# Two heads' products on TensorE issued as one group in five attention stages

## The chip, the cores and the metric

The kernel runs on one core of one Trainium2 chip, as one program. The metric is device time in microseconds (us) of one execution; for the kernel before, the median of three runs is 3418.66 us.

## What is computed

The reference passes a sequence of 512 tokens of width 1024 through three transformer blocks, one after the other. What matters here are the five attentions in which two heads share the 128 rows or the 128 columns of the PE array:

- **fox** (block 1): eight heads of width 64, causal, with a forget-gate bias. A head's scores are `q[64, 128] . k[64, n]` with n = 128, 256, 384 or 512 keys, then a softmax, then the product with the values.
- **da** (block 2, differential attention): eight heads, each with two score maps of contraction 64 over all 512 keys; the second map's softmax is subtracted from the first's with a weight.
- **wa** (block 2, window attention): sixteen heads of width 64 over a window of 256 or 384 keys, with a sink, then `values[128, 64]` products.
- **na** (block 3, neighbourhood attention): eight heads of width 64 over 256 keys, then values.
- **mla** (block 3, latent attention): eight heads with scores of contraction 96 over 512 keys, then values of width 64.

```
s = jnp.einsum('bhqd,bhkd->bhqk', q, k, preferred_element_type=jnp.float32) * scale
p = jax.nn.softmax(...)
o = jnp.einsum('bhqk,bhkd->bhqd', p.astype(v.dtype), v)
```

Around them lie dense projections (each fp32 weight is split into a high and a low part, and three products are summed) and two mixtures of experts.

## The kernel before

The kernel is written with a tile framework. It is traced as straight code without loops at run time; when the program is built, a list scheduler fixes the order of every engine's instructions: of the instructions that are ready in its own model of time it takes the one with the best priority, which is by default the earliest in the trace. On the chip each engine takes its queue in exactly that order. So an instruction of a later dense projection can stand between two instructions of an attention, and work of an earlier part comes ahead of a later part's.

An attention stage is a row of parts, one for each pair of heads and each block of 128 queries; `stagger` runs the first half of part n+1 (scores and softmax) before the second half of part n (transposes and values). In each part:

- `self.sc()` hands out the one score tile in PSUM (`bufs=1`, two banks of 512 floats): head 0's scores go to bank 0, head 1's to bank 1.
- The score products are lines L649 (fox), L1434 (da), L1513 (wa) and L1816 (na). Head 0 uses rows 0 to 63 of the array and head 1 rows 64 to 127; the profile gives such a product the form 64*128. Each fp32 product of the source appears as two MATMUL instructions, so a pair of heads is four.
- `softmax2` reads the scores on VectorE (L459, head 0 and then head 1), takes exponentials on ScalarE (L468), and in wa and na divides on VectorE (L476).
- `transposes` (L433 on TensorE) turns the probabilities; the copies out of PSUM are L436 on VectorE and L438 on ScalarE. In wa and mla one head's copy is on VectorE and the other's on ScalarE; in na both heads come with one copy on ScalarE.
- The value products are L1532 (wa), L1828 (na) and L1930 (mla). Both heads use all 128 rows; head 0 writes from columns 0 to 63 and head 1 from columns 64 to 127 of the array (form 128*64). For each block of 128 keys the source issues head 0 and then head 1. The values of fox (L662) and da (L1447) use the whole array (form 128*128) and are not touched.
- Dense work that the scheduler puts between: L419, L1277 and L383.

In the source the two score products of a part stand next to each other, but nothing keeps other TensorE work from being ordered between them.

Of the kernel before, what the change touches and what calls it, by code (L numbers as in the profile page):

```python
# [35 lines left out]
P = 128  # L36
# [91 lines left out]
class Net:  # L128
# [55 lines left out]

    def pst(self):
        return self.ps.tile([P, 512], F32, name="pst", bufs=2)

    def keep_warm(self, x, n):

# [330 lines left out]
    def mixer1(self):  # L520
# [9 lines left out]
        with ExitStack() as cx:  # L530
# [104 lines left out]
            def fox_part(hp, qt):  # L635
                n = (qt + 1) * P
                if qt == 0:
                    ftab[hp] = tab = A.tile([P, 2, S], F32, name="ftab")
                    for i in range(2):
                        pb = self.pst()  # L640
                        h = 2 * hp + i
                        nc.tensor.matmul(pb, self.ident[:8, h:h + 1].to_broadcast([8, P]), cs[:8], start=True,
                                         stop=True)
                        nc.scalar.activation(tab[:, i], pb, AF.Copy, scale=-1.0)
                tab = ftab[hp]
                sp = self.sc()
                for i in range(2):
                    hs = slice(i * 64, i * 64 + 64)
                    nc.tensor.matmul(sp[:, i, :n], fq[hp][hs, qt * P:n], fk[hp][hs, :n], start=True, stop=False)  # L649
                for i in range(2):  # L650
                    nc.tensor.matmul(sp[:, i, qt * P:n], idb, mb, start=False, stop=True)
                e = A.tile([P, 2, S], F32, name="e", bufs=2)
                _, rl = self.softmax2([e[:, i, :n] for i in range(2)], [sp[:, i, :n] for i in range(2)], 1.0,
                                      tabs=[tab[:, i, :n] for i in range(2)], normalize=False)
                yield
                po = self.pst()
                for i in range(2):
                    h = 2 * hp + i
                    eT = A.tile([P, 4, P], F32, name="eT", bufs=3)
                    self.transposes(eT, e[:, i], qt + 1)  # L660
                    for k in range(qt + 1):
                        nc.tensor.matmul(po[:, i * 64:(i + 1) * 64], eT[:, k], fv[k][:, h * 64:(h + 1) * 64],  # L662
                                         start=(k == 0), stop=(k == qt))
                nc.vector.tensor_mul(y[:, qt, hp * P:(hp + 1) * P].rearrange("p (i d) -> p i d", i=2),
                                     po[:, :P].rearrange("p (i d) -> p i d", i=2),
                                     rl.unsqueeze(2).to_broadcast([P, 2, 64]))
                if qt < 3:
                    return
                o = y[:, :, hp * P:(hp + 1) * P].rearrange("p a (i d) -> p a i d", i=2)
                sq = A.tile([P, 4, 2, 64], F32, name="gy")  # L670
                nc.scalar.activation(sq, o, AF.Square)
                ss = self.small.tile([P, 4, 2], F32, name="ss8")
                nc.vector.reduce_sum(ss, sq, axis=AX.X)
                r = self.power(ss.rearrange("p a i -> p (a i)"), 8, 64, EPS)
                nc.vector.tensor_mul(o, o, r[:, :8].rearrange("p (a i) -> p a i", a=4).unsqueeze(3).to_broadcast([P, 4, 2, 64]))
# [653 lines left out]
    def mixer2(self):  # L1329
# [96 lines left out]
        def da_part(h, qt):  # L1426
            slope = 2.0 ** -(h + 1)
            if qt == 0:
                rows_da[h] = E.tile([P, 4, P], F32, name="oh", bufs=1)
            tab = dist[:, 384 - qt * P:896 - qt * P]  # L1430
            sp = self.sc()
            for m in range(2):
                ms = slice(m * 64, (m + 1) * 64)
                nc.tensor.matmul(sp[:, m], dq[h][ms, qt * P:(qt + 1) * P], dk[h][ms], start=True, stop=True)  # L1434
            e = e_tile()
            l, rl = self.softmax2([e[:, m] for m in range(2)], [sp[:, m] for m in range(2)], slope,
                                  tabs=[tab] * 2, normalize=False)
            c = self.small.tile([P, 1], F32, name="dac")
            nc.vector.scalar_tensor_tensor(c, l[:, 0:1], rl[:, 1:2], nlam, op0=OP.mult, op1=OP.mult)
            nc.vector.scalar_tensor_tensor(e[:, 0], e[:, 1], c, e[:, 0], op0=OP.mult, op1=OP.add)  # L1440
            yield
            oh = rows_da[h]
            eT = E.tile([P, 4, P], F32, name="eT", bufs=3)
            self.transposes(eT, e[:, 0], 4, eng="a")
            po = self.pst()
            for k in range(4):
                nc.tensor.matmul(po[:, :P], eT[:, k], dv[h][:, k], start=(k == 0), stop=(k == 3))  # L1447
            nc.scalar.activation(oh[:, qt], po[:, :P], AF.Copy, scale=rl[:, 0:1])
            if qt < 3:
                return  # L1450
            sq = E.tile([P, 4, P], F32, name="eT", bufs=3)
            nc.gpsimd.tensor_mul(sq, oh, oh)
            ss = self.small.tile([P, 4], F32, name="ss4")
            nc.vector.reduce_sum(ss, sq, axis=AX.X)
            r = self.power(ss, 4, P, EPS)
            nc.vector.tensor_mul(oh, oh, r[:, :4].unsqueeze(2).to_broadcast([P, 4, P]))
            pt = self.pst()
            for a in range(4):
                nc.tensor.transpose(pt[:, a * P:(a + 1) * P], oh[:, a], self.ident)
            o_da[h] = O()  # L1460
            nc.scalar.activation(o_da[h], pt, AF.Copy, scale=sg)
# [41 lines left out]
        def wa_part(c2, i, qt):  # L1503
# [4 lines left out]
            n, t0 = k1 - k0, k0 - (qt * P - P)  # L1508
            nb = n // P
            sp = self.sc()  # L1510
            for j in range(2):
                gs = slice(j * 64, j * 64 + 64)
                nc.tensor.matmul(sp[:, j, :n], wq[c2 * 4 + i][gs, qt * P:(qt + 1) * P], wk[c2][gs, k0:k1],  # L1513
                                 start=True, stop=True)
            e = e_tile()
            self.softmax2([e[:, j, :n] for j in range(2)], [sp[:, j, :n] for j in range(2)],
                          [float(sl[h]) for h in hs], tabs=[wd[:, t0:t0 + n]] * 2,
# [7 lines left out]
            for j in range(2):  # L1525
                self.transposes(eT[j], e[:, j], nb, eng="a" if j else "v")
            po = self.pst()
            for k in range(nb):
                kt = k0 // P + k
                for j in range(2):  # L1530
                    g = 2 * c2 + j
                    nc.tensor.matmul(po[j * 64:(j + 1) * 64, :P], wv[kt // 2][:, kt % 2, g * 64:(g + 1) * 64],  # L1532
                                     eT[j][:, k], start=(k == 0), stop=(k == nb - 1))
            for j, h in enumerate(hs):
                (nc.scalar.copy if j else nc.vector.tensor_copy)(o_wa[h // 2][r0, qt * P:(qt + 1) * P],
                                                                 po[j * 64:(j + 1) * 64, :P])
# [207 lines left out]
    def mixer3(self, after):  # L1744
# [63 lines left out]
        def na_part(hp, j):  # L1808
            if j == 0:
                tabs_na[hp] = na_tabs(hp)  # L1810
            tabs = tabs_na[hp]
            sp = self.sc()
            for hh in range(2):
                hs = slice(hh * 64, hh * 64 + 64)
                kv = k[hp][hs].rearrange("p (i c) -> p i c", c=64)
                nc.tensor.matmul(sp[:, hh, :256], q[hp][hs, j * P:(j + 1) * P], kv[:, :, starts[j]:starts[j] + 32],  # L1816
                                 start=True, stop=True)
            e = N.tile([P, 2, 256], F32, name="ne", bufs=2)
            self.softmax2([e[:, i] for i in range(2)], [sp[:, i, :256] for i in range(2)], 1.0,
                          tabs=[t[:, j].rearrange("p i c -> p (i c)") for t in tabs])  # L1820
            yield
            eT = N.tile([P, 4, P], F32, name="neT", bufs=2)
            self.transposes(eT, e.rearrange("p i k -> p (i k)"), 4, eng="a")
            po = self.pst()
            for kk in range(2):
                for hh in range(2):
                    h = 2 * hp + hh
                    nc.tensor.matmul(po[hh * 64:hh * 64 + 64, :P], vw[j][kk][:, h * 64:(h + 1) * 64],  # L1828
                                     eT[:, hh * 2 + kk], start=(kk == 0), stop=(kk == 1))
            nc.vector.tensor_copy(o_na[hp].rearrange("p (r j c) -> p j r c", j=4, r=8)[:, j],  # L1830
                                  po[:, :P].rearrange("p (r c) -> p r c", r=8))

# [70 lines left out]
        def mla_part(hp, qt):  # L1903
# [20 lines left out]
            for b in range(2):  # L1924
                self.transposes(eT[:, b], e[:, b], 4, eng="a" if b else "v")
            po = self.pst() if hp == 0 else self.acc()
            for kt in range(4):
                for b in range(2):
                    h = 2 * hp + b
                    nc.tensor.matmul(po[b * 64:(b + 1) * 64, :P], mv[:, kt, h * 64:(h + 1) * 64], eT[:, b, kt],  # L1930
                                     start=(kt == 0), stop=(kt == 3))
            nc.scalar.copy(o_ml[hp][:, qt * P:(qt + 1) * P], po[:, :P])

        heads = {}
# [126 lines left out]
```

## Time and profile before

| | |
|---|---|
| Median of 3 runs | 3418.66 us (3416.3 to 3419.46) |
| The profiled execution | 3424.08 us, its span 3422.2 us |
| TensorE busy | 3242.2 us, 95% of the span |
| VectorE, ScalarE busy | 1636.8 us (48%), 1289.1 us (38%) |
| Chain that ended last | PE 75%, DMA 13%, VectorE 6%, ScalarE 2% |

PE is TensorE, DVE VectorE and ACT ScalarE. A row of the timeline has start, duration, engine, line, operation, tiles, form and count; consecutive instructions of one kind are merged into one row. Matmuls are pipelined: a row's duration overlaps the next row's, so what a group costs is read from its start to the next row's start. Idle time before an instruction stands in brackets with what ended it.

### The profile page before, as it was taken

The numbers are of one execution on the slowest core, as the hardware profiler recorded it, in microseconds if no ns is written. First come the engines' busy times: TensorE is split into PE (matmuls) and PEld (weight loads), VectorE is DVE, ScalarE is ACT, GpSimd is POOL, SyncE is SP. The second block draws the span as 40 slices with busy tenths as digits, with TensorE's granted clock in tenths as the row PEclk, the third lists the DMA queues.
The fourth block names the chain that finished last, engine by engine and source line by source line (L and its number), as shares of the span: only waits on it lengthen the run. The fifth ranks groups of instructions, "written<-read, shape, count | busy, mean of one in ns | idle before, by whom it ended". The sixth has DMA issues, their size and how long they took to land.

```text
span 3422.2 us, 41346 instructions
## 1 busy us (share of the span) xinstructions
PE 3242.2 (95%) x15500; PEld 2092.0 (61%) x15500; DVE 1636.8 (48%) x3520; ACT 1289.1 (38%) x2662; POOL 130.4 (4%) x128
## 2 busy tenths in 40 slices
PE   8999989998999999999999998898888999999998
PEld 6777866667767767668634333232224676788886
DVE  5546789998354454656311111011014446573356
ACT  6334658886344353554100000000003344452244
POOL 0010010002000000000000000000000000000000
PEclk9999989999999999999899999999999999999999
DMA  5115479985112212114799999999997312133243
GB/s 169 58 62 141 148 261 376 373 313 199 62 50 72 73 53 87 50 35 171 269 402 420 422 420 422 421 421 423 420 422 272 98 50 68 62 99 99 80 165 137
DMA packets 212938, 713.96 MB, mean 209 GB/s; under 512 B 20144, under 2 KB 28096, under 8 KB 180352
## 3 DMA queue, kind: packets, MB, share of 16 engines
q1 hardware_dynamic: 190272, 668.38, 51.1%
q10 hardware_dynamic: 19520, 32.43, 3.0%
q0 software_dynamic: 2944, 10.49, 1.0%
q8 instruction: 123, 2.02, 0.2%
q14 instruction: 79, 0.65, 0.1%
HBM read 693.68 MB, written 17.56 MB: 208 GB/s over the span
## 4 chain that ended last, share of the span: by engine, by line
PE 75%; DMA 13%; DVE 6%; ACT 2%; issue 1%; POOL 1%; ACTq 0%; SPq 0%; POOLq 0%; DVEq 0%
PE acc L419 23%; PE acc L1662 8%; PE acc L282 7%; PE acc L1085 5%; PE acc L1277 5%; PE acc L1693 3%; PE acc L1107 2%; PE pst L433 2%; DMA xl<-in_w_exp_up_dram 2%; DMA rawx<-in_w_exp_gate_dram 2%; DMA xl<-in_w_exp_down_dram 2%; PE sc L1625 2%; PE acc L367 2%; DMA rawx<-in_w_exp_down_dram 2%; DVE wl L221 1%
## 5 line engine op out<-in xcount | busy, mean ns | idle before, releaser
L221 DVE TENSOR_TENSOR wl<-raw,wh 128x512 fp32r<-128x512 f32 (+3 forms) x910 | 606.6, 683 | 578.0 <-ACT wh L218 525.1
L218 ACT CAST wh<-raw 128x512 fp32r<-128x512 f32 (+3 forms) x910 | 546.5, 612 | 737.8 <-PE acc L419 491.4
L419 PE MATMUL acc<-xh,wh 128*128 128x512 f32 x1072 | 426.4, 398 | 7.1 <-ACT wh L218 5.0
L419 PE MATMUL acc<-xl,wh 128*128 128x512 f32 x1072 | 425.0, 396 | 0.0
L419 PE MATMUL acc<-xh,wl 128*128 128x512 f32 x1072 | 424.4, 396 | 0.0
L1662 PE MATMUL acc<-rawx,xe 128*64 128x512 f32 x1256 | 293.0, 601 | 29.3 <-DMA rawx<-in_w_exp_up_dram 20.9
L419 PEld LDWEIGHTS acc<-xh,wh 128*128 128x128 f32 x1072 | 202.2, 189 | 61.0 <-issue 10.2
L419 PEld LDWEIGHTS acc<-xl,wh 128*128 128x128 f32 x1072 | 202.4, 189 | 51.5 <-issue 13.2
L419 PEld LDWEIGHTS acc<-xh,wl 128*128 128x128 f32 x1072 | 202.2, 189 | 50.4 <-issue 10.8
L1662 PEld LDWEIGHTS acc<-rawx,xe 128*64 128x64 f32 x1256 | 84.2, 137 | 228.2 <-issue 147.7
L1693 PE MATMUL acc<-rawx,wh 128*64 128x512 f32 x640 | 147.0, 599 | 13.1 <-DMA rawx<-in_w_exp_down_dram 13.0
L282 PE MATMUL acc<-wl,xsh 128*128 128x512 f32 x336 | 132.9, 396 | 4.8 <-DVE wl L221 4.7
L207 POOL TENSOR_TENSOR pw_r<-pw_v,halfneg 128x1 f32<-128x1 f32 (+2 forms) x64 | 58.4, 913 | 2053.8 <-DVE pw_v L206 2036.2
L282 PE MATMUL acc<-wh,xsl 128*128 128x512 f32 x336 | 132.2, 394 | 0.0
L282 PE MATMUL acc<-wh,xsh 128*128 128x512 f32 x336 | 128.7, 392 | 0.0
L1662 PE MATMUL acc<-raw,xe 128*64 128x512 f32 x512 | 119.2, 598 | 9.6 <-DMA raw<-in_w_exp_gate_dram 9.6
L1681 DVE SCALAR_TENSOR_TENSOR wl<-wl,acc 128x512 f32<-128x512 f32 x32 | 22.0, 687 | 205.0 <-PE acc L1662 205.0
L468 ACT ACTIVATE e<-e,smx 128x512 f32<-128x512 f32 (+3 forms) x160 | 98.7, 618 | 50.1 <-DVE smx L466 37.3
L438 ACT COPY wh<-pst 128x512 f32<-128x512 f32 x32 | 18.7, 585 | 260.1 <-PE pst L433 260.0
L1693 PEld LDWEIGHTS acc<-rawx,wh 128*64 128x64 f32 x640 | 42.1, 136 | 103.7 <-issue 68.5
L1085 PE MATMUL acc<-wh,xeh 128*96 128x512 f32 x256 | 103.6, 406 | 0.7 <-ACT xeh L218 0.7
L1085 PE MATMUL acc<-wl,xeh 128*96 128x512 f32 x256 | 103.6, 404 | 0.0
(538 smaller groups left out, 5581.3 us busy)
## 6 DMA issues: line engine op xcount, KB each, us to landing
rawx<-in_w_exp_up_dram SPq DMA_DIRECT2D x80, 1024.0 KB
rawx<-in_w_exp_down_dram SPq DMA_DIRECT2D x80, 1024.0 KB
rawx<-in_w_exp_gate_dram SPq DMA_DIRECT2D x77, 1024.0 KB
raw<-in_w_in_dram SPq DMA_DIRECT2D x58, 1024.0 KB
raw<-in_w_exp_gate_dram SPq DMA_DIRECT2D x34, 1024.0 KB
raw<-in_w_exp_down_dram SPq DMA_DIRECT2D x32, 1024.0 KB
raw<-in_w_exp_up_dram SPq DMA_DIRECT2D x30, 1024.0 KB
raw<-in_w_ffn_out_dram SPq DMA_DIRECT2D x22, 1024.0 KB
```

The source lines that it names most:

```text
L218: nc.scalar.copy(hi, src)
L221: nc.vector.tensor_sub(lo, src, hi.bitcast(F32))
L282: nc.tensor.matmul(acc[a, hf], l[:, js], r, start=(k == 0 and q == 0), stop=(k == nk - 1 and q == 2))
L367: self.nc.tensor.matmul(acc[a], l[:, k, js], r[:, :n], start=(k == 0 and q == 0), stop=(k == nk - 1 and q == 2))
L419: nc.tensor.matmul(outs[j], l, r, start=(kk == 0 and q == 0), stop=(kk == nk - 1 and q == 2))
L433: nc.tensor.transpose(pt[:, k * P:(k + 1) * P], src[:, (b + k) * P:(b + k + 1) * P], self.ident)
L468: nc.scalar.activation(es[i], src[i], AF.Exp, bias=nm[:, i:i + 1], scale=sc[i], accum_out=l[:, i:i + 1])
L1085: nc.tensor.matmul(ps, l[:, k], r, start=(k == 0 and q == 0), stop=(k == 7 and q == 2))
L1107: nc.tensor.matmul(py[hf], l[:, k], r, start=(k == 0 and q == 0), stop=(k == 3 and q == 2))
L1277: nc.tensor.matmul(acc[j], l[:, js], r, start=(k == 0 and q == 0), stop=(k == nk - 1 and q == 2))
L1662: nc.tensor.matmul(acc[f // 2][f % 2 * 64:(f % 2 + 1) * 64], cur[:, k, es], raw[f], start=(k == 0), stop=(k == 7))
L1693: nc.tensor.matmul(py[hf * 64:(hf + 1) * 64], uT[ab][:, kk, c * 64:(c + 1) * 64], raw[:, d, hf * 512:(hf + 1) * 512], start=(i + d == 0), ...
```

## The change

A helper `together` takes a list of calls. It makes the first, and then makes the others inside two contexts: `issue_after(mm.ins)` puts an edge of order on TensorE from the first instruction to each of the others (issue order only, no wait for its end), and `high_priority()` gives the others a better priority than any ordinary instruction. It is used for the scores of fox, da, wa and na, each with head 1 first and head 0 behind it, and for the values of wa, na and mla, where for each block of keys head 1 now comes ahead of head 0. The arithmetic, the tiles, the buffers and every other engine's instructions stay. mla's scores, fox's mask product (L651) and the values of fox and da stay as they are.

```diff
+    def together(self, calls):
+        mm = calls[0]()
+        with self.tc.issue_after(mm.ins), self.tc.high_priority():
+            for c in calls[1:]:
+                c()
...
-                for i in range(2):
+                def scores(i):
                     hs = slice(i * 64, i * 64 + 64)
-                    nc.tensor.matmul(sp[:, i, :n], fq[hp][hs, qt * P:n], fk[hp][hs, :n], start=True, stop=False)
+                    return nc.tensor.matmul(sp[:, i, :n], fq[hp][hs, qt * P:n], fk[hp][hs, :n], start=True, stop=False)
+
+                self.together([lambda: scores(1), lambda: scores(0)])
...
-            for k in range(nb):
-                kt = k0 // P + k
-                for j in range(2):
-                    g = 2 * c2 + j
-                    nc.tensor.matmul(po[j * 64:(j + 1) * 64, :P], wv[kt // 2][:, kt % 2, g * 64:(g + 1) * 64],
-                                     eT[j][:, k], start=(k == 0), stop=(k == nb - 1))
+            def values(k, j):
+                g, kt = 2 * c2 + j, k0 // P + k
+                return nc.tensor.matmul(po[j * 64:(j + 1) * 64, :P], wv[kt // 2][:, kt % 2, g * 64:(g + 1) * 64],
+                                        eT[j][:, k], start=(k == 0), stop=(k == nb - 1))
+
+            self.together([lambda k=k, j=j: values(k, j) for k in range(nb) for j in (1, 0)])
```

The scores of da, wa and na change as those of fox do, and the values of na and mla as those of wa.

## Rows read from the trace of the kernel before

**Rows 1.** The profile's page: the span, and the busy time of each engine (share of the span, number of instructions).

```profile
span 3422.2 us, 41346 instructions
...
PE 3242.2 (95%) x15500; PEld 2092.0 (61%) x15500; DVE 1636.8 (48%) x3520; ACT 1289.1 (38%) x2662; POOL 130.4 (4%) x128
```

**Rows 2.** Busy time by stretch: start:end and length in us, then busy us (and instructions) of PE, PEld, DVE, ACT and POOL, the granted clock, the DMA share and GB/s. The stretches are fox with what runs between its parts, two of da, three of wa, one of na and one of mla.

```profile
100.00:260.00 160.00, 158.95 (x854) 112.76 (x852) 84.51 (x231) 54.42 (x124) 12.94 (x10) 0.96 0.18 57
964.00:1037.00 73.00, 69.25 (x321) 41.91 (x320) 47.84 (x133) 38.50 (x93) 6.16 (x6) 1.00 0.09 30
1176.00:1258.00 82.00, 78.34 (x418) 51.58 (x416) 54.63 (x161) 47.96 (x124) 6.14 (x6) 1.00 0.20 65
1302.00:1320.00 18.00, 18.00 (x93) 11.22 (x92) 11.26 (x48) 10.89 (x33) 0.00 (x0) 1.00 0.18 59
1373.00:1436.00 63.00, 63.00 (x343) 37.39 (x342) 41.81 (x161) 37.62 (x118) 0.00 (x0) 1.00 0.06 18
1441.00:1520.00 79.00, 78.93 (x415) 45.45 (x414) 53.63 (x210) 43.41 (x142) 3.00 (x2) 1.00 0.11 37
2694.00:2763.00 69.00, 68.96 (x392) 42.70 (x391) 45.13 (x183) 33.97 (x94) 0.00 (x0) 1.00 0.15 43
2893.00:2952.00 59.00, 54.05 (x367) 35.26 (x366) 34.78 (x72) 26.32 (x69) 0.00 (x0) 0.94 0.02 5
```

**Rows 3.** Timeline of PE in da: a pair of heads in one piece (x4), one in two pieces (x2 and x2, the first such pair of the stage), one behind an idle stretch, and the end of the last pair in two pieces.

```profile
965.40 1.13 PE L1434 MATMUL sc<-qkv 64*128 64x512 f32 x4
966.46 0.50 PE L419 MATMUL acc<-xh,wh 128*128 128x512 f32 x1
966.80 0.39 PE L419 MATMUL acc<-xl,wh 128*128 128x512 f32 x1
967.03 0.40 PE L419 MATMUL acc<-xh,wl 128*128 128x512 f32 x1
...
972.27 1.12 PE L1434 MATMUL sc<-qkv 64*128 64x512 f32 x2
973.33 1.16 PE L1447 MATMUL pst<-qkv,eT 128*128 128x128 f32 x8
974.41 1.12 PE L1434 MATMUL sc<-qkv 64*128 64x512 f32 x2
975.47 0.50 PE L419 MATMUL acc<-xh,wh 128*128 128x512 f32 x1
...
991.80 1.12 PE L1434 MATMUL sc<-qkv 64*128 64x512 f32 x2 [0.73 <-DVE smx L459]
...
1253.88 1.12 PE L1434 MATMUL sc<-qkv 64*128 64x512 f32 x2
```

**Rows 4.** Timeline of PE in wa: one part's scores in two pieces, the values of another part in two pieces (x2 and x6), and the first and the last split of each kind in the stage.

```profile
1308.17 0.91 PE L1513 MATMUL sc<-qkv 64*128 64x384 f32 x2
...
1310.43 0.43 PE L1532 MATMUL pst<-eT,qkv 128*64 128x128 f32 x2
...
1448.85 0.91 PE L1513 MATMUL sc<-qkv 64*128 64x384 f32 x2
1449.69 0.66 PE L433 MATMUL pst<-c_ident,e 128*128 128x128 f32 x4
1450.28 0.91 PE L1513 MATMUL sc<-qkv 64*128 64x384 f32 x2
1451.12 0.43 PE L1532 MATMUL pst<-eT,qkv 128*64 128x128 f32 x2
1451.48 0.50 PE L419 MATMUL acc<-xl,wh 128*128 128x512 f32 x1
1451.81 0.40 PE L419 MATMUL acc<-xh,wl 128*128 128x512 f32 x1
1452.14 0.65 PE L1532 MATMUL pst<-eT,qkv 128*64 128x128 f32 x6
1452.72 0.50 PE L419 MATMUL acc<-xh,wh 128*128 128x512 f32 x1
...
1504.73 0.91 PE L1513 MATMUL sc<-qkv 64*128 64x384 f32 x2
...
1516.30 0.43 PE L1532 MATMUL pst<-eT,qkv 128*64 128x128 f32 x2
```

**Rows 5.** Timeline of PE in na: one piece of a split pair of scores with what follows it, and a part's values in one piece (x8) with what follows them.

```profile
2732.98 0.70 PE L1816 MATMUL sc<-nk,nq 64*128 64x256 f32 x2
2733.60 0.65 PE L433 MATMUL pst<-c_ident,ne 128*128 128x128 f32 x4
...
2735.94 0.66 PE L1828 MATMUL pst<-neT,vw 128*64 128x128 f32 x8
2736.53 0.66 PE L433 MATMUL pst<-c_ident,ne 128*128 128x128 f32 x4
```

**Rows 6.** Timeline of PE in fox: the first half of a split pair of scores over 512 keys, and the values that follow it.

```profile
120.64 1.12 PE L649 MATMUL sc<-t 64*128 64x512 f32 x2
121.69 0.66 PE L662 MATMUL pst<-t,eT 128*128 128x64 f32 x4
```

**Rows 7.** What PE waited for in da (964 to 1260 us): total us, times, longest.

```profile
PE sc L1434 <- DVE smx L459: 3.9, 6, 0.8
```

**Rows 8.** Timeline of DVE in wa: the first read of the scores whose second piece began at 1450.28.

```profile
1451.22 0.56 DVE L459 CUSTOM_DVE_ANT_0 e<-sc,c_wdist 128x384 f32<-128x384 f32 x1 [0.63 <-PE sc L1513]
```

More of the change, by code (lines that the diff above doesn't have):

```diff
@@ L1431, in da_part, with scores @@
             sp = self.sc()
-            for m in range(2):
+            def scores(m):
                 ms = slice(m * 64, (m + 1) * 64)
-                nc.tensor.matmul(sp[:, m], dq[h][ms, qt * P:(qt + 1) * P], dk[h][ms], start=True, stop=True)
+                return nc.tensor.matmul(sp[:, m], dq[h][ms, qt * P:(qt + 1) * P], dk[h][ms], start=True, stop=True)
+            self.together([lambda: scores(1), lambda: scores(0)])
             e = e_tile()
@@ L1510, in wa_part, with scores @@
             sp = self.sc()
-            for j in range(2):
+            def scores(j):
                 gs = slice(j * 64, j * 64 + 64)
-                nc.tensor.matmul(sp[:, j, :n], wq[c2 * 4 + i][gs, qt * P:(qt + 1) * P], wk[c2][gs, k0:k1],
-                                 start=True, stop=True)
+                return nc.tensor.matmul(sp[:, j, :n], wq[c2 * 4 + i][gs, qt * P:(qt + 1) * P], wk[c2][gs, k0:k1],
+                                        start=True, stop=True)
+            self.together([lambda: scores(1), lambda: scores(0)])
             e = e_tile()
@@ L1527, in wa_part @@
             po = self.pst()
-            for k in range(nb):
-                kt = k0 // P + k
-                for j in range(2):
-                    g = 2 * c2 + j
-                    nc.tensor.matmul(po[j * 64:(j + 1) * 64, :P], wv[kt // 2][:, kt % 2, g * 64:(g + 1) * 64],
-                                     eT[j][:, k], start=(k == 0), stop=(k == nb - 1))
+            def values(k, j):
[3 more added lines that the diff above has]
+            self.together([lambda k=k, j=j: values(k, j) for k in range(nb) for j in (1, 0)])
             for j, h in enumerate(hs):
@@ L1812, in na_part, with scores @@
             sp = self.sc()
-            for hh in range(2):
+            def scores(hh):
                 hs = slice(hh * 64, hh * 64 + 64)
                 kv = k[hp][hs].rearrange("p (i c) -> p i c", c=64)
-                nc.tensor.matmul(sp[:, hh, :256], q[hp][hs, j * P:(j + 1) * P], kv[:, :, starts[j]:starts[j] + 32],
-                                 start=True, stop=True)
+                return nc.tensor.matmul(sp[:, hh, :256], q[hp][hs, j * P:(j + 1) * P],
+                                        kv[:, :, starts[j]:starts[j] + 32], start=True, stop=True)
+            self.together([lambda: scores(1), lambda: scores(0)])
             e = N.tile([P, 2, 256], F32, name="ne", bufs=2)
@@ L1824, in na_part, with values @@
             po = self.pst()
[L1825 to L1829, printed above, removed]
+            def values(kk, hh):
+                h = 2 * hp + hh
+                return nc.tensor.matmul(po[hh * 64:hh * 64 + 64, :P], vw[j][kk][:, h * 64:(h + 1) * 64],
+                                        eT[:, hh * 2 + kk], start=(kk == 0), stop=(kk == 1))
+            self.together([lambda kk=kk, hh=hh: values(kk, hh) for kk in range(2) for hh in (1, 0)])
             nc.vector.tensor_copy(o_na[hp].rearrange("p (r j c) -> p j r c", j=4, r=8)[:, j],
@@ L1926, in mla_part, with values @@
             po = self.pst() if hp == 0 else self.acc()
[L1927 to L1931, printed above, removed]
+            def values(kt, b):
+                h = 2 * hp + b
+                return nc.tensor.matmul(po[b * 64:(b + 1) * 64, :P], mv[:, kt, h * 64:(h + 1) * 64], eT[:, b, kt],
+                                        start=(kt == 0), stop=(kt == 3))
+            self.together([lambda kt=kt, b=b: values(kt, b) for kt in range(4) for b in (1, 0)])
             nc.scalar.copy(o_ml[hp][:, qt * P:(qt + 1) * P], po[:, :P])
```

## The prediction

> **What bounds the kernel now.** I read the page first: PE is busy for 3242.2 of 3422.2 us, VectorE for less than half of it [rows 1]. But a share over the whole span is a mean over unlike stages, so next I read the busy time stage by stage [rows 2], and only then the timeline of PE inside the stages that the change touches [rows 3 to 6]. Three kinds of stage are to be seen there. In wa PE has no idle time to speak of (18.00 of 18, 63.00 of 63, 78.93 of 79 us); the same holds for na (68.96 of 69), and fox is close (158.95 of 160). There, a microsecond of PE that is not needed is a microsecond off the end, for dense projections stand ready behind the attention and move up. In da PE is idle for 3.75 of 73 and 3.66 of 82 us: a few waits for the softmax, at the change from one head to the next [rows 2, 3, 7]. In mla it is idle for 4.95 of 59.
>
> **What a pair costs whole and in pieces.** In da, a pair in one piece (x4, all four matmuls of both heads) runs from 965.40 to the next instruction at 966.46, 1.06 us. One head alone (x2) runs from 972.27 to 973.33, again 1.06 us, and the other head, separated by the value products of the part before, from 974.41 to 975.47, once more 1.06 [rows 3]. So two heads side by side take what one takes, and a split pair pays twice. There is also an **edge**: the dense matmul right behind such a block takes 0.34 us to its successor (966.46 to 966.80) where its neighbour takes 0.23 (966.80 to 967.03), 0.11 more [rows 3]; the one right ahead of a block also takes 0.33 (1451.81 to 1452.14 in wa) [rows 4]. One block fewer thus saves up to two edges, 0.2 us, where full-array work stands on both sides, and nothing where another half-array block is the neighbour.
>
> The first rule to hold against this is in the Trainium skill, *TensorE: Matmul & The Clock Gate*, section on packing small matmuls: a weight load overlaps with running matmuls only when its row group differs. That fits the scores, whose heads lie in different rows, but the values of wa, na and mla share all 128 rows and differ in columns alone; by that rule joining them would save nothing. The rows disagree: a lone x2 of values takes 0.36 us (1451.12 to 1451.48), four such would be 1.44, and x8 in na takes 0.59 (2735.94 to 2736.53) [rows 4, 5]. I go by the rows and keep the rule as a rival below.
>
> **The terms, part by part.** The change removes no instruction and adds none; it only closes gaps in PE's order. I counted the split pairs in the timeline and price each by its shape.
>
> - *Fox scores.* 16 parts; those with 384 and 512 keys are all split, 4 + 4. A lone 384 piece is 0.84 us (in wa, 1448.85 to 1449.69 [rows 4]), a lone 512 piece 1.05 (120.64 to 121.69 [rows 6]). 4 x 0.84 + 4 x 1.06 + 8 x 0.2 for edges = 9.2 us.
> - *Da scores.* 14 of 32 pairs are split, the first at 972.27, the last ending with the piece at 1253.88 [rows 3]. 14 x (1.06 + 0.2) = 17.6 us.
> - *Wa scores.* 19 of 32, the first at 1308.17, the last second half at 1504.73: 14 of 384 keys and 5 of 256 [rows 4]. A lone 256 piece is 0.62 (2732.98 to 2733.60, in na [rows 5]). 14 x 1.04 + 5 x 0.82 = 18.7 us.
> - *Wa values.* 30 of 32 parts put head 0's first product (x2) ahead of the rest, from 1310.43 to 1516.30 [rows 4], because its transposed probabilities come first. Price: 0.36 + 0.58 (the x6, 1452.14 to 1452.72) - 0.59 (the x8) = 0.35, and 0.2 of edges where full-array work stands between. In 11 of the 30 a piece touches a score block, so no edge: 19 x 0.55 + 11 x 0.35 = 14.3 us.
> - *Na.* 5 of 16 score pairs of 256 keys are split: 5 x 0.82 = 4.1 us. All 16 value groups are already whole [rows 5]: nothing.
> - *Mla values.* 6 of 16 are split in the same way: 6 x 0.35 = 2.1 us.
>
> On PE this is 66.0 us in all, the upper bound of what shorter PE work can give.
>
> **What of it reaches the end.** Fox and na: all, 9.2 and 4.1, since PE is the bound there and na, whose values are all whole and most of whose pairs are, shows a stage in the new form with PE full [rows 2]. Da: 6 of the 14 split pairs follow an idle wait of PE (such as 991.80 behind 0.73 us of idle; six waits, 3.9 us [rows 3, 7]); there a free PE is worth nothing, so I take the other 8, 10.1 us, with 0 and 17.6 as the ends. Wa: 33.0 us less of 160 leaves 127. VectorE's 106.7 us (11.26 + 41.81 + 53.63) would then be 84% of it, not 67%, so some waits must appear. I let PE idle as much as in da, 3.75 of 73 or 5.1%: 6.5 us, which leaves 26.5. Mla: PE already waits, I take half, 1.0. Sum: 9.2 + 10.1 + 26.5 + 4.1 + 1.0 = **50.9 us**.
>
> What is moved, and what hides it: head 0's product no longer runs as soon as it can. Both products now wait for the later bank, which VectorE gives back one pass later (0.56 us for 384 keys [rows 8]). In PE's queue that wait would stand ahead of everything; the order set at build time puts dense work before it, as around the split pairs now [rows 4]. On the other side a cost goes that the sum doesn't count: VectorE reads the scores only when the second piece is done (the second piece ends at 1451.12, the read starts at 1451.22 after 0.63 us of idle for it [rows 4, 8]), so a pair in one piece releases the softmax earlier. At most this takes away da's whole idle time, 3.75 + 3.66 = 7.4 us. No DMA is issued by the moved work, and SP's and POOL's queues keep their instructions; the dense work that moves up needs its weights earlier, but the DMA share in these stretches is 0.02 to 0.20 [rows 2], so I price that at nothing.
>
> **The rivals.**
>
> - *VectorE and the softmax chain become the bound.* In da, VectorE's share is 66% (47.84 of 73) and PE already waits; wa stands at 67% [rows 2]. If that is the share at which these chains no longer shorten, PE merely idles in da and wa, and fox and na are all that is left: 13.3 us, 3405. For it: VectorE's waits for scores show how tightly the two engines take turns. Against: na at 65% (45.13 of 69) and wa at 67% run with PE full, so the share alone does not force waits. The Trainium skill says the same in *TensorEngine Tiling (Array Packing)*, PSUM bottleneck: tiling speeds up TensorE but not the reading of PSUM, which may become the limit. By that page the time would be this rival's.
> - *Only the values gain nothing,* by the rule on row groups above: the wa values' 14.3 at the 80% that I keep of wa (26.5 of 33.0), 11.5, and mla's 1.0 go: 3380. The x8 row speaks against it [rows 5].
> - *Slower: the front product stalls the queue.* 96 pairs (16 + 32 + 32 + 16) each wait up to one VectorE pass, 0.56 us: 54 us. 48 value groups (32 + 16) wait for the second copy, up to the 1.02 us between the first piece and the rest (1451.12 to 1452.14 [rows 4]): 49 us. If nothing covers these, 103 - 66 = 37 us slower, 3455. It decides from the point at which more than 64% of them (66 of 103) is uncovered. Against: PE now has dense work to put there.
> - *It does not join them.* The edge says "behind", not "next"; if head 0's product is not ready in the order's planning, something else still goes between, and the time stays, 3419.
>
> **How the numbers follow.** The profiled execution took 3424.08 us, 5.4 more than the median of the runs; with 50.9 less it would take 3373.2. On the median: 3418.66 - 50.9 = **3368**. Chances: this case 0.70, the chain as bound 0.14, the values' rule 0.04, nothing joined 0.06, slower 0.06. Low end: all 66.0 of PE and da's 7.4 of idle, 3345. High end: the chain as bound, 3406. That leaves out "nothing joined", "slower" and part of the first rival, some 0.19. A measurement of this kernel can tell about 0.2% (7 us) from no change; by these cases faster has 0.88, the same 0.06, slower 0.06.
>
> **What would show it.** In the timeline of the changed kernel every score block of da, wa, fox and na should be x4 and every value block whole, each as long as a whole block now (1.06 for 512 keys). The stretches of fox, da, wa and na should be shorter by the terms above. PE's idle time in wa should be 3 to 10 us: near zero would mean that I held back too much, above 20 that the softmax chain has taken over. VectorE's waits for L1513 should shrink. It would be wrong if x2 rows remain, or if PE idles ahead of the joined blocks with a VectorE release.

## The result and the profile after

The kernel with the change takes 3378.19 us (median; 3374.8 to 3379.03), the kernel before, timed beside it, 3417.48 (3414.68 to 3419.46): a ratio of 0.9882 [0.9869, 0.9894], 39.3 us faster. The forecast was 50.9 us, 3368, with a range of 3345 to 3406: the sign and the range hold, and the size is 11.6 us too large. The profiled execution of the kernel after took 3379.03 us (its span 3377.0), near its median; that of the kernel before lies 6.6 above its own, so the two spans differ by 45.2.

The lines of code are 8 to 22 further down in the kernel after: scores L657 (fox), L1445 (da), L1527 (wa), L1834 (na); values L1547 (wa), L1848 (na), L1952 (mla); `transposes` L441 with copies L444 (VectorE) and L446 (ScalarE); softmax L467; dense L427; da's transposes at the end of a head L1472 (before: L1459).

The page: span, and busy time of each engine, to be read against [rows 1].

```profile
span 3377.0 us, 41353 instructions
PE 3182.9 (94%) x15500; PEld 2067.6 (61%) x15500; DVE 1634.4 (48%) x3520; ACT 1291.0 (38%) x2662; POOL 130.9 (4%) x128
```

The same 15500 matmuls take 59.3 us less of PE, and the span is 45.2 shorter: PE is idle more than before. Where, the busy times by stretch say (columns as in [rows 2]; the stretches cover about the same parts of da, da, wa, wa, wa, na and mla, as the numbers of instructions show):

```profile
950.40:1025.00 74.60, 64.94 (x320) 42.02 (x319) 47.77 (x133) 39.29 (x93) 6.19 (x6) 0.95 0.09 29
1162.30:1246.00 83.70, 74.57 (x432) 52.53 (x431) 54.85 (x166) 49.86 (x129) 7.19 (x7) 0.98 0.15 51
1288.50:1305.60 17.10, 16.88 (x94) 10.86 (x93) 11.29 (x48) 11.02 (x33) 0.00 (x0) 1.00 0.19 62
1358.60:1410.00 51.40, 49.95 (x340) 32.09 (x339) 41.12 (x161) 37.38 (x118) 0.00 (x0) 1.00 0.06 22
1416.00:1482.50 66.50, 64.28 (x422) 40.81 (x421) 53.73 (x210) 43.93 (x144) 3.00 (x2) 1.00 0.12 40
2652.40:2717.50 65.10, 65.06 (x392) 41.30 (x391) 45.34 (x183) 34.36 (x94) 0.00 (x0) 1.00 0.17 50
2848.00:2906.50 58.50, 50.90 (x358) 31.86 (x357) 33.75 (x72) 26.94 (x69) 0.00 (x0) 1.00 0.02 6
```

In wa, 135 us now do what 160 did, with PE idle for 0.22 + 1.45 + 2.22 = 3.9 us; na is 65.1 for 69 and still full. The two stretches of da are no shorter than before, PE idle there has risen from 3.75 and 3.66 to 9.66 and 9.13 us, and the mean clock is under 1.00.

The timeline of PE in the kernel after: whole blocks in fox and wa.

```profile
116.71 1.13 PE L657 MATMUL sc<-t 64*128 64x512 f32 x4
117.77 0.66 PE L672 MATMUL pst<-t,eT 128*128 128x64 f32 x4
...
1425.99 0.66 PE L1547 MATMUL pst<-eT,qkv 128*64 128x128 f32 x8 [0.56 <-ACT eT L446]
1426.58 0.50 PE L427 MATMUL acc<-xl,wh 128*128 128x512 f32 x1
...
1427.24 0.70 PE L1527 MATMUL sc<-qkv 64*128 64x256 f32 x4
1427.87 0.87 PE L441 MATMUL pst<-c_ident,e 128*128 128x128 f32 x6
```

Each takes from its start to the next row what a whole block, or one half of a split pair, took before: 1.06 us for 512 keys, 0.63 for 256 (a lone half took 0.62 [rows 5]), 0.59 for x8. All 96 score pairs and the 48 value groups of wa and na are in one piece.

To say where the gain arises I take the starts of the n-th matmul on PE in both traces (both have 15500) and give after minus before; a stage's gain is the change of that difference over the stage. The difference at the start of fox (-3.0) stems from the start-up, before any changed instruction.

| Stage | after - before at its start and end, us | gain | forecast |
|---|---|---|---|
| fox and the output projection behind it | -3.0, -13.1 | 10.1 | 9.2 |
| da | -13.75, -13.4 | -0.35 | 10.1 |
| wa | -13.4, -39.7 | 26.3 | 26.5 |
| na | -41.6, -45.7 | 4.1 | 4.1 |
| mla | -45.6, -45.2 | -0.4 | 1.0 |

Outside the changed stages the difference wanders, by up to 3.4 us from one trace to another. The sums of fox, wa and na are near their forecasts, and da's is missing whole. What these sums are made of is told below; in fox and in wa errors of opposite sign cancel.

### The profile page after: what moved, and what is told of

Its sections match the earlier page's. It is cut to its first block, busy times and chain, and to the rows that moved or that the text cites. A ratio compares the mean times of both kernels' runs of the same rounds, so it can differ in the third digit from the quotient of the medians.

```text
span 3377.0 us, 41353 instructions
## 1 busy us (share of the span) xinstructions
PE 3182.9 (94%) x15500; PEld 2067.6 (61%) x15500; DVE 1634.4 (48%) x3520; ACT 1291.0 (38%) x2662; POOL 130.9 (4%) x128
## 4 chain that ended last, share of the span: by engine, by line
PE 53%; DMA 13%; DVE 6%; ACT 3%; issue 1%; POOL 1%; ACTq 0%; POOLq 0%; SPq 0%; DVEq 0%
PE acc L427 19%; PE acc L1679 8%; PE acc L290 5%; PE acc L1287 5%; PE acc L1710 4%; DMA rawx<-in_w_exp_gate_dram 3%; DMA xl<-in_w_exp_up_dram 3%; DMA xl<-in_w_exp_down_dram 3%; PE sc L1642 2%; ACT e L476 2%; PE pst L441 2%; DMA xl<-in_w_exp_gate_dram 1%; PE pst L1719 1%; DMA rawx<-in_w_exp_up_dram 1%; DVE wl L229 1%
## 5 line engine op out<-in xcount | busy, mean ns | idle before, releaser
L427 PE MATMUL acc<-xh,wh 128*128 128x512 f32 x1072 | 426.6, 398 | 7.0 <-ACT wh L226 5.0
L427 PE MATMUL acc<-xl,wh 128*128 128x512 f32 x1072 | 425.9, 397 | 0.0
L427 PE MATMUL acc<-xh,wl 128*128 128x512 f32 x1072 | 423.8, 395 | 0.0
L427 PEld LDWEIGHTS acc<-xh,wh 128*128 128x128 f32 x1072 | 202.9, 189 | 55.7 <-ACT wh L226 7.6
L427 PEld LDWEIGHTS acc<-xh,wl 128*128 128x128 f32 x1072 | 202.8, 189 | 47.0 <-issue 6.7
L427 PEld LDWEIGHTS acc<-xl,wh 128*128 128x128 f32 x1072 | 203.2, 190 | 44.8 <-issue 6.4
L446 ACT COPY wh<-pst 128x512 f32<-128x512 f32 x32 | 18.8, 586 | 259.9 <-PE pst L441 259.9
```

The lines of the kernel that those rows point to most:

```text
L427: nc.tensor.matmul(outs[j], l, r, start=(kk == 0 and q == 0), stop=(kk == nk - 1 and q == 2))
```

## The experiments

Each kernel was timed in five rounds against the kernel before, which took 3419.03 (e1 to e4), 3417.82 (e5 to e8) and 3416.79 us (e9 to e12).

**Is da worth nothing?** e1 is the kernel after with da's scores issued as before.

```diff
-            self.together([lambda: scores(1), lambda: scores(0)])
+            for m in range(2):
+                scores(m)
```

> The changed kernel with da's score pairs issued as before (no helper there); everything else stays changed. Theory A (da gave nothing: what PE saves in the 14 split pairs of da comes back as PE waiting 2.0 to 2.3 us at each change of heads, 18.8 us in all against 7.4 before, and as a lower granted clock after three of those waits): the time stays within 4 us of the changed kernel, 3374 to 3382, and PE's idle time in da falls back to about 7 us. Rival B (da gave its forecast 10 us and something else lost it): about 3388.

3376.76 us (3375.28 to 3381.55), ratio 0.9882 [0.9866, 0.9897], the ratio of the kernel after. Joining da's scores is worth nothing that can be measured; the two intervals leave room for some 7 us, not for the forecast 10.1. What PE waited for in da, first in e1 and then in the kernel after (total us, times, longest; the transposes at a head's end are L1473 in e1, L1472 in the kernel after):

```profile
PE sc L1445 <- DVE smx L467: 3.9, 6, 0.8
PE pst L1473 <- DVE oh L1470: 3.1, 3, 1.8
```

```profile
PE pst L1472 <- DVE smx L481: 6.1, 3, 2.0
PE pst L1472 <- DVE oh L1469: 5.7, 3, 2.1
PE pst L1460 <- ACT eT L446: 3.1, 6, 0.7
...
PE pst L1472 <- DVE dac L1452: 2.3, 1, 2.3
```

e1 has the waits of the kernel before [rows 7]. In the kernel after the wait has moved to L1472, the transposes at the end of a head, 14.1 us in seven waits (an eighth, of 1.4 us, lies behind these rows). Its timeline of PE shows one of them:

```profile
973.43 1.13 PE L1445 MATMUL sc<-qkv 64*128 64x512 f32 x4
974.49 0.50 PE L427 MATMUL acc<-xl,wh 128*128 128x512 f32 x1
974.83 0.40 PE L427 MATMUL acc<-xh,wl 128*128 128x512 f32 x1
975.06 0.39 PE L427 MATMUL acc<-xh,wh 128*128 128x512 f32 x1
977.73 1.05 PE L1472 MATMUL pst<-c_ident,oh 128*128 128x128 f32 x4 [2.27 <-DVE dac L1452]
978.57 1.06 PE L441 MATMUL pst<-c_ident,e 128*128 128x128 f32 x4
979.28 0.78 PE L427 MATMUL acc<-xl,wh 128*128 128x512 f32 x1
979.85 0.63 PE L427 MATMUL acc<-xh,wl 128*128 128x512 f32 x1
```

Before, ten dense products and then the first half of a pair of the next head stood ahead of those transposes, and that half pair took the wait (0.73 us [rows 3]). Now only three dense products stand there, and the transposes wait through the chain that produces `oh` on VectorE. Behind the wait dense products take 0.57 and 0.43 us to the next row (979.28 to 979.85 to 980.28), not 0.23: the busy times by stretch give the granted clock, the last figure but two of the row (the first and the last of three).

```profile
977.78:981.19 3.41, 3.41 (x13) 3.03 (x14) 2.24 (x6) 1.79 (x3) 0.00 (x0) 0.50 0.00 0
...
1230.37:1233.78 3.41, 3.41 (x18) 3.28 (x16) 1.47 (x6) 1.16 (x4) 0.00 (x0) 0.50 0.59 195
```

Three stretches of 3.41 us are at half, the 1.2 GHz level, each beginning within 1.3 us of the end of a PE wait of 1.9 to 2.3 us at a head's end; the kernel before has none in da. By an estimate from these rows they cost up to 3 x 1.7 = 5.1 us.

**What if the first pair of each head is left as it was?** The prediction took the 8 split pairs without a wait of PE ahead of them as full gain. e2 joins the pairs of queries 128 and up of each head. That does not pick out the 8: it takes in six of them, and also all six pairs that stood behind a wait, which are the third of their heads (queries 256 to 383).

```diff
+            if qt:
                 self.together([lambda: scores(1), lambda: scores(0)])
+            else:
+                for m in range(2):
+                    scores(m)
```

> The changed kernel, but in da the first part of each head (query block 0) has its score pair issued as before; the other three parts of each head stay joined. Theory A (the wait at the head change is what eats da's gain, because head 0's product of the next head no longer stands ahead of the transposes L1472 to fill it): PE's wait there falls from 2.0 us each to under 1 us, the low-clock stretches in da go, and the time is 3366 to 3373, 6 to 12 us below the changed kernel. Rival B (da is bound by VectorE and ScalarE, any order gives the same): 3375 to 3381.

3378.62 us (3377.5 to 3384.32), 0.9887 [0.9872, 0.9902]: no gain, and theory A's number is missed. The wait that it was to take away is still there. The clock is at full in da here, so the low stretches alone are not the cause; PE's idle time in da's two halves is 16.0 us, against 7.4 before and 18.8 in the kernel after. One wait at a head's end (L1476 here) in the timeline, and PE's largest waits in da:

```profile
977.88 0.63 PE L1476 MATMUL pst<-c_ident,oh 128*128 128x128 f32 x4 [2.27 <-DVE dac L1456]
...
PE pst L1476 <- DVE oh L1473: 7.6, 4, 2.3
PE pst L1464 <- ACT eT L446: 3.7, 7, 0.8
```

**Are the transposes at a head's end the culprit?** e5 is the kernel after with these transposes, and the copy behind them, issued one part later in the source; e6 is e5 with da's scores as before.

```diff
-            pt = self.pst()
-            for a in range(4):
-                nc.tensor.transpose(pt[:, a * P:(a + 1) * P], oh[:, a], self.ident)
-            o_da[h] = O()
-            nc.scalar.activation(o_da[h], pt, AF.Copy, scale=sg)
+            def finish():
+                pt = self.pst()
...
+            pend.append(finish)
```

> The changed kernel with one thing more: in da, the four transposes at the end of a head (of its normed output) are issued one part later, behind the values of the next head's first part. Theory A (the wait for the norm's chain on VectorE and GpSimd at each change of heads takes da's gain): PE's 12.4 us of waits there and the three low-clock stretches of da go, and the time falls by 8 to 15 us, to 3363 to 3370. Rival B (the softmax chain of VectorE and ScalarE bounds all of da, so PE waits elsewhere): 3374 to 3380.

> The same later transposes, but da's score pairs issued as in the kernel before (the rest stays changed). It is the partner of the run with da joined. Theory A: with the head change out of the way, joining da's pairs is worth most of its 17.6 us of PE work, so this one is 8 to 17 us slower than its partner, about 3375. Rival B: within 4 us of its partner.

e5 took 3378.99 us (3371.29 to 3383.77), 0.9888 [0.9872, 0.9905]; e6 3379.22 (3373.37 to 3381.12), 0.989 [0.9875, 0.9905]. The waits of e5:

```profile
PE pst L1476 <- DVE oh L1471: 6.2, 4, 1.8
PE pst L1457 <- ACT eT L446: 5.4, 7, 1.1
PE sc L1443 <- DVE smx L467: 4.4, 10, 1.3
```

The wait at the transposes is smaller, two half-level stretches of 3.41 us are still there, and waits reappear at the values and the scores. Rival B's times are what came in both runs: whichever instruction is taken out of the way, the next one waits. (e6 is a rough partner, with 10 of da's 32 pairs split and not 14.) Rival B's reason, that the softmax chain bounds all of da, does not follow from that.

**What PE does with the time.** From the traces, da's second half (first to last score product), by what PE issued: its time from start to next start less idle, with the number of dense products.

| us | before | e1 | after | e2 | e5 |
|---|---|---|---|---|---|
| length | 77.9 | 78.0 | 70.6 | 71.7 | 65.1 |
| scores | 24.5 | 24.5 | 17.0 | 19.1 | 18.2 |
| idle | 3.7 | 3.7 | 9.1 | 8.2 | 8.1 |
| dense products | 149 | 149 | 105 | 114 | 78 |

The scores do take 7.5 us less (and 7.5 in the first half: 15.0, where I had 17.6). And the softmax chain was not what set the length of this half before: it gets through in 70.6 and even 65.1 us instead of 77.9. But fewer dense products are placed in it, and PE waits while there is work: the 44 dense products missing here are issued behind da, where they cost PE time. So da's attention ends earlier there, and the stage together with its dense work does not. In the first half neither the length (117 us) nor the number of dense products (277) changes, and PE is idle for 6.0 us more.

For the whole stage with its dense work, from its first score product to wa's first, the account closes: in the kernel after PE takes 15.1 us less for scores, is idle for 11.7 us more (22.0 for 10.3), and takes 4.6 us more for the same 1008 dense products, near the cost of the half-level stretches; with small differences in the rest the stage is 0.35 us longer.

**Is wa worth its 26.5, and what of it are the values?** e4 has the change in wa alone, e7 in wa's scores alone, e8 in wa's values alone; all other calls of the helper are plain loops as in the kernel before. Of e8:

```diff
-            for k in range(nb):
-                kt = k0 // P + k
-                for j in range(2):
...
+            self.together([lambda k=k, j=j: values(k, j) for k in range(nb) for j in (1, 0)])
```

> The kernel before with only wa changed (its scores and its values through the helper); fox, da, na and mla are as before. Theory A (wa's gain is its own, 25 us of the 33 that PE saves): 25 us below the kernel before, 3390 to 3395. Rival B (part of what the trace shows in wa was carried over from dense work that da left undone): 15 to 20 us below, 3397 to 3403.

> The kernel before with wa's score pairs alone joined. By the prediction's prices 18.7 us of PE work at about 80%: 15 us below the kernel before, 3404. If wa's gain came from the values alone: 3417 to 3421; if the scores bring all of it: 3394.

> The kernel before with wa's value products alone joined. By the prediction's prices 14.3 us at about 80%: 11 us below the kernel before, 3408. By the rule that weight loads overlap only across row groups: no gain, 3417 to 3421.

| | us | ratio | gain, timed, us | gain, wa in the trace, us |
|---|---|---|---|---|
| e4, both | 3394.46 (3390.76 to 3396.84) | 0.9926 [0.9912, 0.994] | 24.6 | 26.4 |
| e7, scores | 3402.8 (3399.11 to 3406.38) | 0.996 [0.9947, 0.9974] | 15.0 | 16.5 |
| e8, values | 3399.63 (3396.92 to 3400.37) | 0.9946 [0.9933, 0.996] | 18.2 | 16.5 |

By the intervals a timed gain is known to some 4.5 us here, so 15.0 and 18.2 do not differ; the traces give 16.5 for each. Alone they give 33 us, together 24.6 to 26.4. Part of the difference is counted twice: each change also moves the order of the other kind. e7 leaves 23 value groups cut where the kernel before had 30, and its value products take 1.2 us less; e8 leaves 17 score pairs split, not 19, and its scores take 2.1 us less. The rest is PE's waiting, in the busy times of nearly the whole stage, one row each from e7, e8 and e4 (PE idle 0.70, 0.11 and 3.41 of 190 us):

```profile
1290.00:1480.00 190.00, 189.30 (x1021) 130.46 (x1020) 120.07 (x408) 102.95 (x291) 6.00 (x4) 1.00 0.19 62
```

```profile
1290.00:1480.00 190.00, 189.89 (x1018) 130.77 (x1017) 120.78 (x409) 101.62 (x290) 6.00 (x4) 1.00 0.19 62
```

```profile
1290.00:1480.00 190.00, 186.59 (x1066) 131.50 (x1065) 125.09 (x424) 105.59 (x304) 5.99 (x4) 1.00 0.19 62
```

e8 also settles the rival on row groups: products that share all rows of the array gain from standing together too. The values take 10.9 us less of PE in its trace, and the work beside them 3.6 less. The rule in the Trainium skill, *TensorE: Matmul & The Clock Gate*, section on packing small matmuls, that a weight load overlaps only when its row group differs, would, as the prediction read it, have made e8 equal to the kernel before; these runs don't agree with it for the values.

**What do the order and the priority do?** In wa alone again: e9 puts head 0 in front (scores and values), e10 leaves `high_priority()` out of the helper.

```diff
-            self.together([lambda: scores(1), lambda: scores(0)])
+            self.together([lambda: scores(0), lambda: scores(1)])
```

```diff
-        with self.tc.issue_after(mm.ins), self.tc.high_priority():
+        with self.tc.issue_after(mm.ins):
```

> The kernel before with wa alone through the helper, but head 0 in front of head 1, in its scores and its values. Theory A (the scores are held together by the priority, whichever head leads, while the values need the head in front whose copy lands last): score pairs whole, most value groups again split in x2 and the rest, and the time is that of the run with wa's scores alone, 15 us below the kernel before, 3400 to 3406. Rival B (the front makes no difference): 25 us below, 3391 to 3396.

> The kernel before with wa alone through the helper, head 1 in front, but without the better priority for the products behind it (the edge of order alone). Theory A (the edge alone lets the transposes of the part before step in between two scores, but with the last operand in front the values need no priority): most score pairs split, value groups whole, and the time is that of the run with wa's values alone, 18 us below the kernel before, 3397 to 3402. Rival B (the edge does all of it): 25 us below, 3391 to 3396.

e9 took 3401.15 us (3399.43 to 3404.2), 0.995 [0.9938, 0.9963]; e10 3400.56 (3395.99 to 3403.42), 0.995 [0.9937, 0.9962]: 15.6 and 16.2 us of e4's 24.6; in the traces wa gains 16.5 and 16.4 of 26.4. Rows of the timeline of PE, first e9, then e10:

```profile
1443.81 0.43 PE L1549 MATMUL pst<-eT,qkv 128*64 128x128 f32 x2
1444.18 0.50 PE L427 MATMUL acc<-xh,wh 128*128 128x512 f32 x1
...
1444.84 0.87 PE L1549 MATMUL pst<-eT,qkv 128*64 128x128 f32 x10
```

```profile
1432.79 0.91 PE L1529 MATMUL sc<-qkv 64*128 64x384 f32 x2
1433.63 0.66 PE L441 MATMUL pst<-c_ident,e 128*128 128x128 f32 x4
1434.22 0.91 PE L1529 MATMUL sc<-qkv 64*128 64x384 f32 x2
```

In e9 every score pair is whole, but 23 of 32 value groups are cut behind head 0's first product (in one of the other nine PE waits 0.43 us at that place for the ScalarE copy of head 1). In e10 all values are whole, and 17 of 32 score pairs are in two pieces. These are the counts of e7 and e8: with the wrong front the helper does nothing for the values, and without the priority nothing for the scores. So in wa the values need the late operand in front, and the scores need the priority; neither is enough for both.

**Fox, and mla's front.** e12 has the change in fox's scores alone.

```diff
+                self.together([lambda: scores(1), lambda: scores(0)])
-                for i in range(2):
...
```

> The kernel before with fox's score pairs alone joined. By the prediction 9.2 us, 3408 to 3410. By the trace of the changed kernel, which gains 8 us between fox's first part and the dense work behind the mixer and 5 us more at the first product of its output projection: up to 13 us, 3405. If the second is a matter of the clock and not of fox: 3410.

3406.22 us (3399.25 to 3417.64, eight runs that lie wide apart), 0.9967 [0.9954, 0.9979]: 10.6 us; its trace gives 10.2. Only half of it arises in fox. The busy times of fox in the kernel before and in the kernel after, over the same 833 matmuls:

```profile
104.00:260.00 156.00, 154.95 (x833) 109.50 (x832) 81.37 (x226) 52.77 (x122) 12.94 (x10) 0.96 0.18 58
```

```profile
101.00:252.00 151.00, 149.76 (x833) 108.01 (x832) 81.40 (x225) 52.99 (x122) 12.95 (x10) 0.93 0.17 60
```

That is 5.0 us, and 5.0 in e12's trace, not 9.2. The granted clock has fallen from 0.96 to 0.93 there: 20.5 us are at half level in every trace with fox's pairs joined, 13.7 in that of the kernel before, by an estimate 3.4 us of time. The other 5.2 us arise behind fox: in the kernel before, PE waits at the output projection and the clock falls once more; with fox's pairs joined neither is there. The wait of PE before, the busy times of this stretch before, and the stretch in e12:

```profile
PE acc L282 <- ACT wh L218: 2.9, 1, 2.9
```

```profile
258.00:308.50 50.50, 46.80 (x268) 34.19 (x269) 29.65 (x66) 16.88 (x31) 4.55 (x4) 0.97 0.31 98
```

```profile
260.00:310.00 50.00, 49.24 (x267) 36.74 (x267) 32.35 (x66) 21.59 (x36) 4.94 (x5) 1.00 0.52 133
```

e3 is the kernel after with head 0 in front in mla's values, and e11 is e3 with da's scores as before, the version that the runs up to then pointed to.

```diff
-            self.together([lambda kt=kt, b=b: values(kt, b) for kt in range(4) for b in (1, 0)])
+            self.together([lambda kt=kt, b=b: values(kt, b) for kt in range(4) for b in (0, 1)])
```

> The changed kernel, but mla's value products have head 0 in front of head 1 in each block of keys. In the changed kernel 11 of 16 value groups of mla are split, 6 were before: head 1's copy, on ScalarE, is there first in most parts, so head 1 in front goes ahead alone. Theory A (the front must be the head whose operand comes last, and mla is bound by its softmax chain): 4 to 6 groups split, PE's 7.1 us of waits for ScalarE's copies shrink, and the time moves by at most 3 us, 3375 to 3380. Rival B (mla lost its forecast 1 us and more through the split groups, 11 x 0.35 us): 3372 to 3374.

> The changed kernel with da's score pairs as in the kernel before and mla's values with head 0 in front: the two parts that the runs so far show to be worth nothing or better the other way. If their differences add: 3376.8 - 2.6 = 3374, 3 to 5 us below the changed kernel; if they were chance, 3376 to 3379.

e3 took 3375.57 us (3371.6 to 3376.26), 0.9874 [0.9859, 0.9889]; e11 3376.52 (3374.44 to 3380.92), 0.9876 [0.9862, 0.989]. Both lie within what can be told from the kernel after. Why mla gained nothing, the timeline of PE in the kernel after shows, and PE's waits in this stage beside it:

```profile
2870.48 0.43 PE L1952 MATMUL acc<-eT,mv 128*64 128x128 f32 x2 [0.67 <-ACT eT L446]
2870.84 1.12 PE L1940 MATMUL acc<-mkT,mqT 96*128 96x512 f32 x2
2871.90 1.09 PE L1952 MATMUL acc<-eT,mv 128*64 128x128 f32 x14
```

```profile
PE acc L1952 <- ACT eT L446: 7.1, 10, 0.7
```

Head 1 in front cuts more here: its ScalarE copy is the first to end (2870.43; the other at 2870.86), so its first product goes alone, and 11 of 16 groups are cut, against 6 before. With head 0 in front, in e3 and e11, 6 are. Yet the trace of e3 gains 2.8 us in mla over the kernel before and that of e11 none, with the same pieces. The clock differs: the stretch at half level, in the kernel before, e3 and e11.

```profile
2889.36:2899.61 10.25, 9.57 (x34) 5.82 (x35) 5.62 (x13) 3.48 (x10) 0.00 (x0) 0.50 0.00 0
```

```profile
2840.70:2844.10 3.40, 3.40 (x11) 2.08 (x9) 2.53 (x6) 0.41 (x2) 0.00 (x0) 0.50 0.00 0
```

```profile
2846.16:2856.40 10.24, 9.56 (x34) 5.82 (x35) 5.53 (x13) 3.40 (x10) 0.00 (x0) 0.50 0.00 0
```

The kernel after has no such stretch in mla (1.00 above) and pays for five more cuts instead (5 x 0.36 = 1.8 us, and PE idle for 2.5 us more over the stage): the two nearly cancel. That head 0 in front is worth something by itself is therefore not shown.

## Why the prediction was right, and where it was too large

- *What a split pair costs* held for the blocks themselves. In wa the score products take 14.6 us less of PE (14 x 0.84 + 5 x 0.62 = 14.9 by the prediction's prices) and the values 10.9 (30 x 0.35 = 10.5); in da the scores take 15.1 less (14 x 1.06 = 14.8). Na came out (4.1, 4.1).
- *The edges* were priced too high in wa: 19 x 0.2 for scores and 19 x 0.2 for values make 7.6 us, and the transposes and dense products there take 4.6 less. So PE's work in wa fell by 30.1 us, not 33.0.
- *Wa's 6.5 us of idle time* was too much as well: PE is idle for 3.8 us more, inside the 3 to 10 that I named as a sign. The two errors of some 3 us cancel, so that 26.3 in the trace (24.6 timed alone) for 26.5 is partly luck. VectorE's waits for the scores shrank, as the prediction said they should; they are shown before and after:

```profile
DVE e L459 <- PE sc L1513: 11.3, 11, 2.0
```

```profile
DVE e L467 <- PE sc L1527: 0.9, 1, 0.9
```

- *Fox's 9.2 us* came by luck: 5.0 in fox, where the lower clock took about 3.4, and 5.2 behind it, from a wait and a half-level stretch that the prediction did not name.
- *Da's 10.1 us* is the step that failed: "the other 8" pairs were to be full gain, because PE does not wait ahead of them. All 14 together were worth nothing (e1), nor was a set with six of these 8 in it (e2). I read PE's waits as places; they are a sum that the order spreads out. PE does spend 15.1 us less on da's scores, and gets it back as 11.7 us of idle time and 4.6 us of dense products at the lower clock. The low end that I had given this term, 0, is what came. The rival "the chain is the bound" gives this number for da, but its reason is not borne out in the second half, which did get shorter (77.9 to 70.6 us, 65.1 in e5). In wa that rival fell (3405 would have needed none of the 24.6).
- *Mla's 1.0 us* came out as -0.4, with "every value block whole" wrong there: more blocks are cut than before, since the copies end in the other order than in wa.
- *The values' rule, the stalled queue, nothing joined*: e8, the 3.9 us of idle time in wa, and the x4 rows speak against each. That the values' rule gave 3380, nearer to the measured 3378 than my 3368, is chance: it had da at its forecast 10.1 and the values at nothing, and the runs show the reverse.

The parts now make the whole: fox 10.6 + wa 24.6 + na 4.1 + da 0 + mla 0 = 39.3 us, the time measured. Fox and wa are timed alone and known to some 4 us each, and na stands as in the trace, so that the sum fits this closely is partly luck; the table of the traces adds up to 39.8. It stays open why the order set at build time puts fewer dense products between da's pairs once they are joined: that its model sees the waits for VectorE shorter than they are would explain it, but this was only argued.

## What to carry to other kernels

Two products that use half of the PE array each cost one only if nothing stands between them in PE's queue, so count the split pairs in the timeline and price each at a whole block. Where PE is full and stays full the count is the gain (na); in wa, with two kinds of cuts, it was 26 of 33. Where PE already waits for the softmax, price the joining at nothing until a run shows otherwise: the time went into other waits and a lower clock here. Put in front the product whose operands come last by the trace of that stage (which copy ends later), not by the head's number: in wa the wrong front of the values cost 9 us.

## What was not expected of the hardware

- After three of the waits of PE at the end of a head in da (1.9 to 2.3 us) the granted clock was 0.50 for 3.41 us; after the five others (1.4 to 2.1 us) it was not, and e2 kept 1.00 behind a wait of 2.27 us ahead of the same instruction. The kernel before, whose longest wait at such a place was 1.7 us, kept 1.00 in da; e7, where da is as before, had one such stretch, and PE's nearest waits ahead of it were 0.5 and 0.2 us. So the length of the wait alone does not tell. In mla the same pieces of work were granted a half-level stretch of 10.24 us in one trace and of 3.40 in another, 2.8 us of time.
- Products of two heads that differ in array columns only (128*64) run side by side as those that differ in rows do: 0.59 us for x8 where a lone x2 takes 0.36, and wa's values, 30 of 32 groups cut before and none in e8, take 10.9 us less of PE.
